# Layer 2 of a hybrid decoder on one core: S5's kernel taps on quarters of the array, and the input projection begun with three tiles over all tokens

## The chip, the cores and the metric

The kernel runs on one core of a Trainium2 chip. The metric is the device time of one execution in microseconds, as the median of several runs.

## What is computed

Two layers of a decoder over 544 tokens (a prompt of 512 and 8 samples of 4), model width 1024, all in float32. Cut to what matters here:

```python
mod = jax.nn.silu(c) @ w['w_mod'] + w['b_mod']
sh1, sc1, g1, sh2, sc2, g2 = jnp.split(mod[:, None, :], 6, axis=-1)
h = _rmsnorm(x, w['norm1_g']) * (1 + sc1) + sh1
z = h @ w['w_in']
zq, zk, zv, zu, za, zg = jnp.split(z, [o1, o2, o3, o4, o5], axis=-1)
...
bu_re = jnp.einsum('gpc,blgc->blgp', bb_re, u)
bu_im = jnp.einsum('gpc,blgc->blgp', bb_im, u)
acc_r, acc_i, sb_r, sb_i = lax.associative_scan(_complex_affine_combine, (a_re, a_im, bu_re, bu_im), axis=1)
...
y = jnp.einsum('gcp,blgp->blgc', c_re, h_re) - jnp.einsum('gcp,blgp->blgc', c_im, h_im)
y = y + d_skip * u
```

Each layer has this mixer (attention with a window of 128, an S5 state-space group of 256 channels, a convolution group of 256 channels, one output projection) and a SwiGLU feed-forward part (FFN) with a width of 2816.

## The kernel before

**Matmuls.** Activations stand with channels on the partitions and tokens on the free axis, in two halves of 272 tokens. Every weight and every activation is split into a high and a low part, and a product is three matmuls of 128x272 (`mm3`, line 603: high by high, high by low, low by high; in the trace their weights are called hi_s and lo_s). A weight chunk of 512 KB arrives as raw_s; `split` (line 584) casts it to hi_s and subtracts for lo_s, on ACT or DVE and on DVE or GpSimd (POOL). Each output tile of 128 columns and one half takes a PSUM bank, and `mtiles` (line 608) goes through the contraction (k) on the outside, over its halves and tiles inside.

**Input projection.** `project(ms)` (line 1090) computes the column tiles in `ms`. With three tiles it runs one stretch over both halves, in six banks; otherwise a stretch over the first half and one over the second. `STEPS` (line 219) sets, for each layer, in which steps the tiles are projected and where the S5, convolution (c0, c1) and attention parts stand among them; `COLS` names the tiles. In layer 2 the tiles 0, 1, 2 are u0 and u1 (S5's input) and q4 (the keys), 3 and 4 belong to the convolution.

**What the projection needs first.** `stat_tile` (line 685) squares a tile of x on ACT (w_s<-x) and adds it to acc_s; `rstd_of` (line 712) sums acc_s over the channels with one-column matmuls, goes through a chain of 12 small operations on DVE (rs_s, three columns wide) and broadcasts the result over the partitions with three matmuls (ps_s<-cst,rs_s), once for each half. `make_h` (line 734) then makes the projection's activations: a product on DVE (w_s<-x,ps_s), scale and shift on ACT, a cast on ACT and a subtraction on DVE, for each k and half. The scale and shift come from w_mod by the adaLN matmuls (mod_s<-wm_s,silu_c), done in steps of four that are spread over the program; their weights (wm_s) are loaded two chunks at a time.

**S5's parameters.** `ssm_params(l)` (line 816) makes the matrices of S5 from the parameters; layer 2's are made during layer 1's FFN. Its last part, `taps` (line 926), computes the kernel taps kk, a table of 128x128 (position and channel, by channel), from mb (two tables of eight 128x128 blocks) and the columns ctr and nct (16 per block): a pair of accumulating matmuls for each block, with the block as weights and 16 columns moving. The result is added to the skip term dm and masked into the weights ssm_tp; then mb is transposed (16 transposes) into ssm_v.

**Order.** All operations are recorded, and a planner (`_schedule`, line 225) puts them in one order by ranks, modelled costs, the tables above and the slots of its buffers. Each engine and DMA queue then runs its own instructions in that order; none overtakes another. Where the planner's model has PE idle for 60 ns or more, it issues a matmul of zeros (a fill, mod_s<-cst,zeros). All operations have line L111 in the trace, so they are told apart by names. PE runs a plain float32 matmul as two records in the trace, a transpose and the split matmuls as one.

## Time and profile before

| | |
|---|---|
| median of 3 runs | 1311.04 us (1310.49 to 1311.4) |
| the profiled execution's own time | 1313.35 us |
| its span in the profile | 1311.5 us (mean granted TensorE clock 0.994) |
| PE busy | 1295.5 us, 99% of the span |
| DVE, ACT, POOL busy | 723.6 us (55%), 431.5 us (33%), 368.6 us (28%) |

The profile is one execution on the chip. A timeline row gives the start and the length of a group of like instructions that follow each other; an x at the row's end counts them, and brackets give the idle time before the group with what ended it. Records of PE overlap, since matmuls are pipelined: what a group costs is read from its start to the next row's start.

### The profile page before, as it was taken

The numbers are of one execution on the slowest core, as the hardware profiler recorded it, in microseconds if no ns is written. First come the engines' busy times: TensorE is split into PE (matmuls) and PEld (weight loads), VectorE is DVE, ScalarE is ACT, GpSimd is POOL, SyncE is SP. The second block draws the span as 40 slices with busy tenths as digits, with TensorE's granted clock in tenths as the row PEclk, the third lists the DMA queues.
The fourth block names the chain that finished last, engine by engine and source line by source line (L and its number), as shares of the span: only waits on it lengthen the run. The fifth ranks groups of instructions, "written<-read, shape, count | busy, mean of one in ns | idle before, by whom it ended". The sixth has DMA issues, their size and how long they took to land.

```text
span 1311.5 us, 25293 instructions
## 1 busy us (share of the span) xinstructions
PE 1295.5 (99%) x10328; PEld 1219.6 (93%) x10328; DVE 723.6 (55%) x1674; ACT 431.5 (33%) x928; POOL 368.6 (28%) x455
## 2 busy tenths in 40 slices
PE   8999999999999999999999999999999999999997
PEld 7888768999999999999988897899999999999997
DVE  6868884676743357433447868657434323344343
ACT  4533471453221122212226346345312112122232
POOL 8653220248432033322012412022223202233101
PEclk9998999999999999999999999999999999999999
DMA  9886785523222223223366672231232222232322
GB/s 333 288 278 210 235 235 197 182 101 97 97 83 96 81 81 97 95 75 105 108 213 233 229 279 69 95 99 49 97 97 96 82 81 83 95 97 81 97 65 69
DMA packets 79654, 176.56 MB, mean 135 GB/s; under 512 B 22769, under 2 KB 40497, under 8 KB 79537
## 3 DMA queue, kind: packets, MB, share of 16 engines
q1 hardware_dynamic: 79536, 174.94, 40.6%
q8 instruction: 81, 1.33, 0.4%
q14 instruction: 37, 0.30, 0.1%
HBM read 164.22 MB, written 10.70 MB: 133 GB/s over the span
## 4 chain that ended last, share of the span: by engine, by line
PE 90%; DVE 3%; DMA 2%; POOL 2%; issue 1%; SPq 1%; ACT 1%; POOLq 0%; ACTq 0%; DVEq 0%
PE ps_s L111 86%; PE mod_s L111 4%; DVE pg_s L111 2%; POOL sp_s L111 1%; SPq L111 1%; POOL pg_s L111 1%; DVE sp_s L111 1%; DMA raw_s<-w_in 1%; DMA wm_s<-w_mod 1%; DMA pg_s<-d_s 0%; DMA conv_out<-pg_s 0%; ACT pg_s L111 0%; DMA pg_s<-ssm 0%; POOL w_s L111 0%; POOLq L1743 0%
## 5 line engine op out<-in xcount | busy, mean ns | idle before, releaser
L111 PE MATMUL ps_s<-pg_s,hi_s 128*128 128x272 f32 x5504 | 1050.8, 290 | 1.4 <-DVE pg_s L111 1.1
L111 PEld LDWEIGHTS ps_s<-pg_s,hi_s 128*128 128x128 f32 x5504 | 865.1, 189 | 18.6 <-issue 13.8
L111 PE MATMUL ps_s<-pg_s,lo_s 128*128 128x272 f32 x2752 | 791.2, 289 | 0.0
L111 PEld LDWEIGHTS ps_s<-pg_s,lo_s 128*128 128x128 f32 x2752 | 518.7, 189 | 7.0 <-issue 6.9
L111 POOL TENSOR_TENSOR lo_s<-raw_s,hi_s 128x1024 fp32r<-128x1024 f32 x77 | 223.3, 2903 | 657.8 <-DVE hi_s L111 372.0
L111 ACT ACTIVATE hi_s<-raw_s 128x1024 fp32r<-128x1024 f32 x128 | 135.0, 1059 | 356.2 <-PE ps_s L111 313.6
L111 DVE TENSOR_TENSOR lo_s<-raw_s,hi_s 128x1024 fp32r<-128x1024 f32 x95 | 119.7, 1261 | 63.9 <-ACT hi_s L111 62.4
L111 DVE TENSOR_TENSOR pg_s<-w_s,pg_s 128x272 fp32r<-128x272 f32 x148 | 113.3, 775 | 37.4 <-ACT pg_s L111 37.0
L111 PE MATMUL ps_s<-pg_s,pg_s 128*128 128x104 f32 (+10 forms) x864 | 123.5, 317 | 2.9 <-DVE nmx_s L111 1.7
L111 ACT ACTIVATE w_s<-ps_s 128x272 f32<-128x272 f32 (+1 forms) x178 | 69.0, 388 | 165.0 <-PE ps_s L111 145.6
L111 PEld LDWEIGHTS ps_s<-pg_s,pg_s 128*128 128x128 f32 (+4 forms) x864 | 97.1, 182 | 27.5 <-issue 12.5
L111 DVE CAST hi_s<-raw_s 128x1024 fp32r<-128x1024 f32 x44 | 30.4, 695 | 157.0 <-PE ps_s L111 157.0
L111 DVE SCALAR_TENSOR_TENSOR x<-ps_s,modT_s,x 128x272 f32<-128x272 f32 (+1 forms) x96 | 45.8, 482 | 105.9 <-PE ps_s L111 105.7
L111 ACT ACTIVATE pg_s<-w_s 128x272 fp32r<-128x272 f32 x149 | 61.7, 426 | 85.0 <-DVE w_s L111 82.6
L111 DVE TENSOR_TENSOR w_s<-w_s,ps_s 128x272 f32<-128x272 f32 x88 | 38.2, 434 | 69.9 <-ACT w_s L111 69.8
L111 ACT ACTIVATE pg_s<-ps_s 128x512 f32<-128x512 f32 (+11 forms) x100 | 35.2, 382 | 65.3 <-PE ps_s L111 63.5
L111 ACT ACTIVATE w_s<-x 128x272 f32<-128x272 f32 x70 | 29.0, 427 | 69.1 <-DVE x L111 61.3
L111 PE MATMUL mod_s<-wm_s,silu_c 128*32 128x512 f32 x320 | 46.9, 616 | 1.4 <-DMA wm_s<-w_mod 1.4
L111 DVE TENSOR_TENSOR acc_s<-acc_s,w_s 128x272 f32<-128x272 f32 x64 | 34.1, 548 | 18.4 <-ACT w_s L111 17.5
L111 POOL TENSOR_TENSOR acc_s<-acc_s,w_s 128x272 f32<-128x272 f32 x5 | 4.6, 912 | 138.8 <-ACT w_s L111 138.7
L111 ACT ACTIVATE w_s<-w_s,modT_s,gain_s 128x272 f32<-128x272 f32 (+1 forms) x64 | 35.9, 591 | 14.3 <-DVE w_s L111 11.3
L111 DVE TENSOR_TENSOR pg_s<-pg_s,pg_s 128x256 f32<-128x256 f32 (+4 forms) x78 | 37.8, 540 | 0.5 <-ACT pg_s L111 0.3
(139 smaller groups left out, 795.3 us busy)
## 6 DMA issues: line engine op xcount, KB each, us to landing
wm_s<-w_mod SPq DMA_DIRECT2D x80, 512.0 KB, 4.6
raw_s<-w_gate SPq DMA_DIRECT2D x44, 512.0 KB, 3.5
raw_s<-w_up SPq DMA_DIRECT2D x44, 512.0 KB, 3.9
raw_s<-w_down SPq DMA_DIRECT2D x44, 512.0 KB, 3.5
raw_s<-w_in SPq DMA_DIRECT2D x24, 512.0 KB, 6.1
pg_s<-cwt SPq DMA_DIRECT2D x20, 512.0 KB, 6.1
pg_s<-w_mod SPq DMA_DIRECT2D x32, 256.0 KB, 6.0
raw_s<-w_out SPq DMA_DIRECT2D x16, 512.0 KB, 4.0
```

Source lines behind the costliest of these rows:

```text
L111: r = real(*a, **k)
```

## The change

Two tables of code change. In layer 2 `taps` exchanges the operands of its matmuls: the 16 columns of ctr or nct, together with the 16 columns of the neighbouring block, are the weights (32 columns, on one quarter of the array, so that the result lands on 32 of 128 PSUM partitions), and the block of mb moves with 128 columns. Four such matmuls on the four quarters are kept together (`order.glue`). The result stands the other way round, so it is copied into a page and transposed back (two transposes of 128x128), and the blocks that count are added to dm in three pieces. The first entry of layer 2's `STEPS` becomes (0, 1, 2), so the projection begins with three tiles over all tokens, where tiles 0 and 1 were projected one by one and half by half, and tile 2 behind the S5 part. The planner's test for free slots is written another way, with the same meaning.

```diff
-         ((0,), (1,), "s5", (2,), (3, 4), "c0", (5,), (6,), (7,), (8,), (9,), "attn", (10, 11), "c1", "norm"))
+         ((0, 1, 2), "s5", (3, 4), "c0", (5,), (6,), (7,), (8,), (9,), "attn", (10, 11), "c1", "norm"))
...
         def taps():
 
-            kp = mbank()
-            for gp in range(8):
-                o = kp[:, gp * 16:(gp + 1) * 16]
-                PE.matmul(out=o, lhsT=mb[0][:, gp].rearrange("p s h c -> p (s h c)"), rhs=ctr[:, gp, :], start=True, stop=False)
-                PE.matmul(out=o, lhsT=mb[1][:, gp].rearrange("p s h c -> p (s h c)"), rhs=nct[:, gp, :], start=False, stop=True)
+            if l == 0:
...
+            else:
+
+                kp = mbank()
+                for b2 in range(2):
+                    for i, c in enumerate((ctr, nct)):
+                        order.glue = ("taps", kp.tensor.name, b2, i)
+                        for q4 in range(4):
+                            gp = 4 * b2 + q4
+                            g0 = min(gp, 6)
+                            PE.matmul(out=kp[32 * q4:32 * q4 + 32, b2 * P:(b2 + 1) * P], lhsT=c[:, g0:g0 + 2, :].rearrange("p g c -> p (g c)"),
+                                      rhs=mb[i][:, gp].rearrange("p s h c -> p (s h c)"), start=i == 0, stop=i == 1, skip_group_check=True)
+                        order.glue = None
+                kt = tmp[0].rearrange("p g s c -> p (g s c)")[:, :2 * P]
+                cp(kt, kp[:, :2 * P])
+                kp = mbank()
+                for b2 in range(2):
+                    PE.transpose(kp[:, b2 * P:(b2 + 1) * P], kt[:, b2 * P:(b2 + 1) * P], ident)
...
-            tt(kk, kp[:, :128], dm, ADD)
+            if l == 0:
+                tt(kk, kp[:, :128], dm, ADD)
+            else:
+                for b2 in range(2):
+                    v = kp[:, b2 * P:(b2 + 1) * P].rearrange("p (g h c) -> p g h c", g=4, h=2)
+                    o = 4 * b2
+                    for g0, m, hh_ in ((0, 4, 0),) if b2 == 0 else ((0, 3, 0), (3, 1, 1)):
+                        d_ = slice((o + g0) * 16, (o + g0 + m) * 16)
+                        tt(kk[:, d_].rearrange("p (g c) -> p g c", c=16), v[:, g0:g0 + m, hh_], dm[:, d_].rearrange("p (g c) -> p g c", c=16), ADD)
```

Since the planner decides, the order moves from the end of layer 1's FFN to the end of layer 2's mixer. PE has 121 fills in place of 104.

PE between the end of layer 1's FFN and the first projection matmuls of layer 2, before: the taps (128x16) with single projection matmuls (128x272) between them, then three fills and the first half's stretch. The broadcast of the second half (rs_s) comes 17 rows behind this piece.

```order
L111 MATMUL ps_s_794_1218<-pg_s_788_646,pg_s_790_633 128x16
L111 MATMUL ps_s_794_1218<-pg_s_752_626,pg_s_789_630 128x16
L111 MATMUL ps_s_1162_1228<-pg_s_1093_1221,hi_s_1079_1175 128x272
L111 MATMUL ps_s_794_1218<-pg_s_788_646,pg_s_790_633 128x16
L111 MATMUL ps_s_794_1218<-pg_s_752_626,pg_s_789_630 128x16
L111 MATMUL ps_s_1200_1230<-pg_s_1093_1221,hi_s_1144_1186 128x272
L111 MATMUL ps_s_794_1218<-pg_s_788_646,pg_s_790_633 128x16
L111 MATMUL ps_s_794_1218<-pg_s_752_626,pg_s_789_630 128x16
L111 MATMUL ps_s_794_1218<-pg_s_788_646,pg_s_790_633 128x16
L111 MATMUL mod_s_0_135<-cst,zeros 128x128 x3
L111 MATMUL ps_s_1157_1223<-pg_s_1093_1221,hi_s_1074_1170 128x272
L111 MATMUL ps_s_1157_1223<-pg_s_1093_1221,lo_s_1075_1173 128x272
```

The same place now, from behind the taps (32x128): fills, the second half's sums (acc_s), the two new transposes, the first half's broadcast, eight fills, an adaLN step, the second half's broadcast, then the projection.

```order
L111 MATMUL ps_s_794_1205<-pg_s_790_633,pg_s_788_646 32x128 x4
L111 MATMUL mod_s_0_135<-cst,zeros 128x128 x2
L111 MATMUL ps_s_1123_1211<-cst,acc_s_561_1118 128x1 x3
L111 MATMUL ps_s_795_1212<-cst,pg_s_787_767 128x128 x2
L111 MATMUL mod_s_0_135<-cst,zeros 128x128 x3
L111 MATMUL ps_s_1102_1188<-cst,rs_s_1104_1203 128x128 x2
L111 MATMUL ps_s_1102_1188<-cst,rs_s_1104_1203 128x16
L111 MATMUL mod_s_0_135<-cst,zeros 128x128 x8
L111 MATMUL mod_s_0_135<-wm_s_1409_1195,silu_c 32x512 x2
L111 MATMUL mod_s_0_135<-wm_s_1410_1196,silu_c 32x512 x2
L111 MATMUL ps_s_1123_1211<-cst,rs_s_1125_1215 128x128 x2
L111 MATMUL ps_s_1123_1211<-cst,rs_s_1125_1215 128x16
```

Both broadcasts now stand ahead of the first projection matmul, and 13 fills stand here.

ACT at the end of layer 1's FFN, before (hi_s_1144 is the cast of the third w_in chunk, hi_s_1160 that of the fourth, w_s_1091<-x_83 the last square of the second half):

```order
L111 ACTIVATE w_s_1088_1184<-x_82 128x272
L111 ACTIVATE hi_s_1144_1186<-raw_s_1143_1176 128x1024
L111 ACTIVATE w_s_1091_1204<-x_83 128x272
L111 ACTIVATE pg_s_748_1197<-ps_s_795_1196 128x512
L111 ACTIVATE hi_s_1160_1210<-raw_s_1159_1181 128x1024
```

and now (1145 and 1159 are these two casts, w_s_1092 the square):

```order
L111 ACTIVATE w_s_1089_1182<-x_82 128x272
L111 ACTIVATE hi_s_1145_1186<-raw_s_1144_1176 128x1024
L111 ACTIVATE hi_s_1159_1197<-raw_s_1158_1179 128x1024
L111 ACTIVATE w_s_1092_1206<-x_83 128x272
L111 ACTIVATE pg_s_748_1192<-ps_s_796_1191 128x512
```

The fourth chunk's cast stands ahead of the square instead of behind it. On DVE that chunk's subtraction (lo_s) now stands ahead of the last add of the second half (acc_s); here is what follows there, the second half's chain (rs_s_1124 to 1126) beside the taps' three adds (pg_s_788) and the first masked copies:

```order
L111 TENSOR_SCALAR rs_s_1124_1213<-ps_s_1123_1211 128x3
L111 SCALAR_TENSOR_TENSOR rs_s_1104_1203<-rs_s_1105_1204,rs_s_1104_1203 128x3
L111 TENSOR_SCALAR rsi_s_1127_1214<-rs_s_1124_1213 128x3
L111 TENSOR_TENSOR pg_s_788_646<-ps_s_795_1212,pg_s_788_646 128x64
L111 TENSOR_SCALAR rs_s_1125_1215<-rsi_s_1127_1214 128x3
L111 TENSOR_TENSOR pg_s_788_646<-ps_s_795_1212,pg_s_788_646 128x48
L111 TENSOR_TENSOR pg_s_788_646<-ps_s_795_1212,pg_s_788_646 128x16
L111 SCALAR_TENSOR_TENSOR rs_s_1126_1216<-rs_s_1124_1213,rs_s_1125_1215 128x3
L111 TENSOR_SCALAR pg_s_745_622<-pg_s_788_646,cst 32x8x16
L111 TENSOR_TENSOR rs_s_1126_1216<-rs_s_1126_1216,rs_s_1125_1215 128x3
L111 TENSOR_SCALAR pg_s_745_622<-pg_s_788_646,cst 32x8x16
L111 SCALAR_TENSOR_TENSOR rs_s_1125_1215<-rs_s_1126_1216,rs_s_1125_1215 128x3
```

Before, the sums and this chain came ahead of the taps' add, and the chain ran beside the first half's products.

## Rows read from the trace of the kernel before

**Rows 1.** The page: the span, and busy time of each engine.

```profile
span 1311.5 us, 25293 instructions
...
PE 1295.5 (99%) x10328; PEld 1219.6 (93%) x10328; DVE 723.6 (55%) x1674; ACT 431.5 (33%) x928; POOL 368.6 (28%) x455
```

**Rows 2.** Windows: us, busy us (instructions) of PE, PEld, DVE, ACT, POOL; PEclk, DMA, GB/s.

```profile
500.00:600.00 100.00, 100.00 (x801) 100.00 (x800) 44.45 (x67) 20.90 (x39) 28.02 (x10) 1.00 0.26 85
...
685.73:689.15 3.42, 3.42 (x34) 3.42 (x33) 2.33 (x7) 3.25 (x6) 1.71 (x1) 1.00 0.95 287
689.15:692.56 3.41, 3.41 (x32) 3.41 (x32) 3.41 (x13) 3.41 (x9) 3.04 (x8) 1.00 0.94 317
692.56:695.97 3.41, 3.41 (x18) 3.41 (x17) 3.21 (x10) 3.15 (x8) 1.13 (x2) 0.50 0.70 284
```

**Rows 3.** Timeline of PE: start us, us, line, operation, out<-in, xcount.

```profile
676.25 1.07 PE L111 MATMUL mod_s<-wm_s,silu_c 128*32 128x512 f32 x8
677.25 0.52 PE L111 MATMUL ps_s<-pg_s,hi_s 128*128 128x272 f32 x2
...
683.65 1.88 PE L111 MATMUL mod_s<-wm_s,silu_c 128*32 128x512 f32 x8
685.46 0.66 PE L111 MATMUL ps_s<-cst,pg_s 128*128 128x128 f32 x4
...
686.54 0.82 PE L111 MATMUL ps_s<-cst,rs_s 128*128 128x128 f32 x6
687.21 0.85 PE L111 MATMUL ps_s<-cst,pg_s 128*128 128x128 f32 x6
687.90 1.86 PE L111 MATMUL ps_s<-pg_s,pg_s 128*128 128x16 f32 x16
...
691.77 0.91 PE L111 MATMUL mod_s<-cst,zeros 128*128 128x128 f32 x6
692.44 0.47 PE L111 MATMUL ps_s<-pg_s,hi_s 128*128 128x272 f32 x1
...
696.05 0.29 PE L111 MATMUL ps_s<-pg_s,lo_s 128*128 128x272 f32 x1
```

**Rows 4.** Timeline of PE at the kernel's start: a modulation group on quarters.

```profile
13.67 0.64 PE L111 MATMUL mod_s<-pg_s,silu_c 128*32 128x128 f32 x16
14.24 0.83 PE L111 MATMUL ps_s<-cst,acc_s 128*128 128x1 f32 x6
```

**Rows 5.** Timelines of SyncE and ACT, and the landing times of raw_s in 660 to 700 us.

```profile
678.25 0.38 SPq L111 DMA_DIRECT2D raw_s<-w_in  x1
...
684.06 0.43 ACT L111 ACTIVATE w_s<-x 128x272 f32<-128x272 f32 x1 [3.49 <-DVE rs_s L111]
...
686.32 1.05 ACT L111 ACTIVATE hi_s<-raw_s 128x1024 fp32r<-128x1024 f32 x1
...
DMA to landing us min/median/max: 3.4/5.5/7.5
```

**Rows 6.** Timeline of DVE at the same place.

```profile
680.60 1.23 DVE L111 TENSOR_TENSOR lo_s<-raw_s,hi_s 128x1024 fp32r<-128x1024 f32 x1 [0.51 <-ACT hi_s L111]
682.24 0.16 DVE L111 TENSOR_SCALAR rs_s<-ps_s 128x3 f32<-128x3 f32 x1 [0.41 <-PE ps_s L111]
...
684.52 0.44 DVE L111 TENSOR_TENSOR acc_s<-acc_s,w_s 128x272 f32<-128x272 f32 x1
```

**Rows 7.** Timelines of PE and DVE: S5, and the attention's wait.

```profile
726.11 0.29 PE L111 MATMUL ps_s<-pg_s,lo_s 128*128 128x272 f32 x1
726.51 3.94 PE L111 MATMUL ps_s<-pg_s,pg_s 128*128 128x136 f32 x32
...
754.64 3.94 DVE L111 TENSOR_TENSOR pg_s<-pg_s,pg_s 128x256 f32<-128x256 f32 x10
...
794.48 0.70 PE L111 MATMUL ps_s<-pg_s,pg_s 64*128 64x256 f32 x2 [0.82 <-DVE nmx_s L111]
```

**Rows 8.** The page's groups: PE's small matmuls; busy, mean, idle before and its releaser.

```profile
L111 PE MATMUL ps_s<-pg_s,pg_s 128*128 128x104 f32 (+10 forms) x864 | 123.5, 317 | 2.9 <-DVE nmx_s L111 1.7
```

More of the change, by code (lines that the diff above doesn't have):

```diff
@@ L338, in _schedule, with placeable @@
     lock = {}
+    needs = [[(n, tags[n][0], nth[n]) for n in t] for t in touch]
+    def placeable(i):
+        for n, t, m in needs[i]:
+            if n not in held:
+                f = len(free[t])
+                if not f or f <= RESERVE.get(t, 99) and f <= bisect.bisect_left(todo[t], m):
+                    return False
+        return True
     pick, why, last_dep, slot_by, freed_by, prev_end, prev_op = [0] * N, {}, {}, {}, {}, {}, {}
@@ L365, in _schedule @@
                 for r, i in pool[e]:
-                    if not all(len(free[tags[n][0]]) > min(bisect.bisect_left(todo[tags[n][0]], nth[n]), RESERVE.get(tags[n][0], 99))
-                               for n in touch[i] if n not in held):
+                    if not placeable(i):
                         continue
@@ L387, in _schedule @@
                         best = (key, r, i, p)
+                    if e != "ACT":
+                        break
                 if best is None and e == "PE" and FILL and spare and NWU <= issued < reals and now >= at[e] + (0.0 if filled else FILL):
@@ L926, in taps @@
         def taps():
-            kp = mbank()
-            for gp in range(8):
-                o = kp[:, gp * 16:(gp + 1) * 16]
-                PE.matmul(out=o, lhsT=mb[0][:, gp].rearrange("p s h c -> p (s h c)"), rhs=ctr[:, gp, :], start=True, stop=False)
-                PE.matmul(out=o, lhsT=mb[1][:, gp].rearrange("p s h c -> p (s h c)"), rhs=nct[:, gp, :], start=False, stop=True)
+            if l == 0:
+                kp = mbank()
+                for gp in range(8):
+                    o = kp[:, gp * 16:(gp + 1) * 16]
+                    PE.matmul(out=o, lhsT=mb[0][:, gp].rearrange("p s h c -> p (s h c)"), rhs=ctr[:, gp, :], start=True, stop=False)
+                    PE.matmul(out=o, lhsT=mb[1][:, gp].rearrange("p s h c -> p (s h c)"), rhs=nct[:, gp, :], start=False, stop=True)
+            else:
[11 more added lines that the diff above has]
+                cp(kt, kp[:, :2 * P])
+                kp = mbank()
+                for b2 in range(2):
+                    PE.transpose(kp[:, b2 * P:(b2 + 1) * P], kt[:, b2 * P:(b2 + 1) * P], ident)
             kk = bb[:, 512:640]
```

## The prediction

> **What bounds the kernel now.** I read the page's summary first: TensorE (PE) is busy 99% of the span [rows 1]. So time is saved only by giving PE less to do, by letting it run at its higher clock, or by removing one of its few waits; VectorE (DVE) and ScalarE (ACT) matter only where PE comes to wait for them. Next the table by windows [rows 2]: in 500 to 600 us PE issues 801 matmuls in 100 us, 0.125 us each, with no gap. The three windows behind it show the place of this change: the granted clock is 1.00 until 692.56 and 0.50, the lower of the two levels, from there to 695.97 where layer 2's input projection begins. What PE did before the clock fell stands in its timeline [rows 3]: transposes, one-column sums, and the 16-column tap matmuls. Three sizes are read there, each as the distance from a start to the next row's start:
>
> - The taps. From 687.90 to 691.77, less three stray projection matmuls of 0.125: 3.5 us for 32 records, 0.11 each.
> - The half clock. From 692.44 to 696.05, 16 projection matmuls in 3.61 us; at 0.125 they take 2.0. Lost: 1.6 us.
> - A late load of w_mod. The eight records at 683.65 last 1.81 us; the same eight at 676.25 last 1.00. Lost: 0.8 us.
>
> The profiled execution took 1313.35 us with a span of 1311.5, and lies 2.3 above the median of 1311.04. I sum the change against it and take the difference over to the median. About 0.2%, 2.6 us, is what a measurement can tell from no change.
>
> **The change part by part.**
>
> *Taps.* The 16 instructions (32 records) with 16 moving columns go: -3.5. In their place come 16 with 32 columns of weights, 128 moving columns, on quarters of the array. No row of before has them with these operands; the nearest is the modulation at the kernel's start, also 32 columns of weights and 128 moving, where a group of 16 records lasts 0.64 us [rows 4], so 32 take 1.3. The bounds are 1.1 (the next row starts 0.57 after that group's start) and 3.5 (quarters do not overlap, 0.11 each as in the old taps). I take 1.3, since shape and tiling are the same. The sum for this part: -2.2. The Trainium skill, "TensorEngine Tiling (Array Packing)", Performance Considerations, gives up to 4 times for a swap of the two operands with at most 32 columns; by it the taps would take an estimated 0.9 and the total would come out 0.4 lower. No run has shown that yet.
>
> *Copy, transposes and adds.* Two more transposes on PE at 0.115 (from 687.21 to 687.90, six records) [rows 3]: +0.2. The copy out of PSUM is one more ACT operation. It lies beside PE's fills and the second half's sums, so I cost it at nothing; without that cover it would be about 0.4, as ACT's square of nearly the same size [rows 5]. The three adds in place of one are two more operations on DVE; where they stand is counted with DVE below.
>
> *Fills.* The order has 17 more zero matmuls (121 for 104): 13 before the first projection matmul, where 4 stood around there, 9 at the end of S5, where 2 stood, and one later. One takes 0.22 (three from 691.77 to 692.44 [rows 3]): +3.8. They are issued whether or not there is anything to wait for, so I count all of them as work and below only what a wait lasts beyond them.
>
> Work: -2.2 + 0.2 + 3.8 = **+1.8**.
>
> *What goes of the old losses.* The half clock came right after the 16-column taps, and these are gone: -1.6. The bounds are 0 and -1.6; I take the whole, since the granted clock was still 1.00 behind the transposes at 685.46 and 687.21 and the broadcast between them [rows 2, 3]. The late w_mod: in the new order the step at this place uses a pair of chunks whose loads stand one earlier in the queue: -0.8 (0 if the next w_mod pair, now behind the hist and rope transfers, is late instead). Together **-2.4**.
>
> *What is late next: the start of the projection.* Before, PE could begin with the first half's tokens while the second half's statistics were still being made. Now three tiles run over all tokens, and the order puts the broadcast of the second half's rstd ahead of the first projection matmul. That needs the last square (ACT), the last add into acc (DVE), three one-column sums (PE) and the chain of 12 small operations (DVE). On ACT the cast of the fourth w_in chunk now stands ahead of that square, and on DVE its subtraction ahead of the add. The step by step: this chunk was issued at 678.25 and its cast began at 686.32 [rows 5]; the queue landed such chunks in 3.4 to 7.5 us, so it lands between 681.7 and 685.8, and I take 684, near the median of 5.5. Cast 1.05 to 685.05, subtraction 1.23 to 686.3, add 0.44 to 686.7 [rows 5, 6]; the rest of the first half's chain, six operations at 0.2 that wait on each other (682.24 is such a one), to 687.9. Then 24 DVE operations from the second chain's start to its end, with the taps' three adds and five normalisations between. They last from 0.16 (as 682.24) to 0.44 (as 684.52) and overlap in pairs; I estimate 0.19 each, 4.6 us, to 692.5. Broadcast 0.67 (686.54 to 687.21), so the projection starts at 693.2.
>
> By PE's own work it would start as follows. The FFN ended at 682.9 (683.65 less six transposes). Less 1.0 for the adaLN step that leaves the FFN's last tiles (as at 676.25), and 0.4 for the first sums, counted next: 681.5. Then two sets of sums at 0.6 (685.46 to 686.54, less four transposes), 18 transposes 2.1, taps 1.3, 13 fills 2.9, two adaLN steps 2.0, two broadcasts 1.3: 10.8, to 692.3. The wait is the difference: **+0.9**, with the bounds 0 (the chunk lands at 681.7, and PE's own work sets the time) and +2.7 (685.8).
>
> *DVE and ACT inside the stretch.* With six banks a k step lasts 18 matmuls, 2.3 us, and each needs both halves' activations: four DVE operations of 0.4 [rows 6], four on ACT of the same order, with the weights' casts between. That is nearly as long. I take **+0.5** (0 to 1).
>
> *S5's end.* The DVE chain from the first copy to its last row (754.64 + 3.94) ends 32 us after the first input matmul of S5 at 726.51 [rows 7]. In the new order PE has about 5 us less work between that matmul and the first outputs; the first outputs need only groups that DVE finishes before its last scans, the last set needs the end. With the nine fills counted, PE gets there about when DVE ends: **+0.3** (0 to 1).
>
> Total: 1.8 - 2.4 + 0.9 + 0.5 + 0.3 = +1.1: 1314.4 for an execution like the profiled one, **1312.1** on the median.
>
> **The rivals.**
>
> *Faster: no new wait.* The chunk lands near 681.7, DVE keeps ahead in the stretch, S5 ends in time, and the wait of 0.82 that PE has for the softmax maximum [rows 7] goes with its smaller companions (1.7 in all in the page's group [rows 8]), as the query tiles shift; so does the 0.3 by which 726.51 comes later than 0.125 after 726.11 [rows 7]. Then -0.6 - 1.7 - 0.3 = -2.6: 1308.4. For it: PE hardly waited anywhere before. Against it: the order shows a longer chain ahead of the first matmul, and fills mark where gaps are expected. Chance 0.20, of which some 0.12 goes beyond the bound.
>
> *Slower: head of the line.* The fourth chunk lands as late as before or later. ACT and DVE run in order, so the square and the add behind the cast and the subtraction wait with them, though the three tiles don't need that chunk at all. At 685.8 the start moves by 1.8 more: 1313.9; at 687, 1315.1. It decides from a landing later than about 685.5. For it: DMA was moving 317 GB/s there, 0.94 busy [rows 2]. Against it: 7.5 is the longest of its stretch. Chance 0.18, at 1314.3.
>
> *The clock falls all the same.* The gap of the new order still has 18 transposes, one-column sums, and waits. If the first 16 projection matmuls again run at 0.226, the 1.6 is not gained: 1313.7. Rows speak against it (clock 1.00 through the old transposes). The Trainium skill, "TensorE: Matmul & The Clock Gate", Part 4 (PE-mode transpose), says that a transpose does not count as PE being busy in the same way; by it the gap would be thinner than it looks and the low level would return. The trace agrees in so far only as the clock did fall after this stretch, though not right behind the transposes. Chance 0.08.
>
> *The change doesn't do what it says.* The quarters run one after another and the new taps cost the old 3.5: 2.2 more, 1314.3. Against it: the row for the same shape. Chance 0.06.
>
> **How the numbers follow.** Forecast 0.48, rivals 0.20, 0.18, 0.08 and 0.06. The range runs from 1308.4, the faster rival's time, to 1315.6, past the late chunk's. Faster than 1308.4: 0.13, nearly all the first rival. Slower than 1313.7: 0.13 from the late chunk, 0.04 from the clock, 0.05 from the quarters and 0.03 from the forecast's own upper end: 0.25. Same: 0.62.
>
> **What would show it.** In the profile of the changed kernel: taps as 32 records within 1.3 us; 242 records of fills; a granted clock of 1.00 through the first projection matmuls; PE idle before the second half's broadcast or the first projection matmul, released by DVE's rs_s or pg_s; the cast of the fourth chunk ahead of the last square on ACT; short waits of the S5 outputs for DVE. The forecast is wrong if PE has no gap there (faster), if the cast starts after 685.5 (slower), or if the clock shows 0.50 again.

## The result and the profile after

| | before | after |
|---|---|---|
| median of runs taken side by side | 1311.22 us (4 runs, 1310.49 to 1312.08) | 1321.55 us (4 runs, 1320.07 to 1322.87) |
| the profiled execution's own time | 1313.35 us | 1320.07 us |
| its span (mean granted TensorE clock) | 1311.5 us (0.994) | 1318.3 us (0.998) |

The ratio is 1.0068, with an interval of 1.0051 to 1.0085. The change makes the kernel 10.3 us slower by the medians and 8.9 by the ratio (6.7 to 11.1). That lies within 2%, but far outside the 0.2% that the prediction called no change, and above its range.

The page of the changed kernel, its span and the busy time of each engine:

```profile
span 1318.3 us, 25379 instructions
...
PE 1298.1 (98%) x10364; PEld 1220.7 (93%) x10364; DVE 728.3 (55%) x1678; ACT 431.2 (33%) x927; POOL 369.3 (28%) x455
```

Against [rows 1], PE has 36 more records: 17 fills (two records each) and two transposes. It is busy for 2.6 us more, in a span that is 6.8 us longer. So most of the loss is PE waiting.

The two profiled executions differ before the changed place too. At 98 to 106 us the granted clock was 0.57 in the one of before and 1.00 in the one of after. The order there is the same in both, so this isn't the change. After reaches the end of layer 1's FFN (its first one-column sums) at 679.83, before at 681.10. From there to the span's end after takes 638.5 us and before 630.4: the change costs 8.1 us in these two executions.

To see where, I cut this part at the starts of rows that both traces have: the first sums at the FFN's end, the first S5 input matmul (128x136), the first S5 output, the first convolution matmul (128x104), layer 2's first FFN sums, and PE's last record. In each stage I summed what PE issues at the durations that undisturbed rows show (0.125 a matmul with 272 columns, 0.22 a fill, 1.0 an adaLN step). The stage's time less that sum is what PE lost, to waits and to the clock:

| lost, us | start and first stretch | S5's input to its first output | to the convolution | to layer 2's FFN | the FFN | sum | PE's work |
|---|---|---|---|---|---|---|---|
| before | 3.2 | 0.6 | 1.9 | 3.2 | 2.0 | 11.0 | 612.1 |
| after | 5.1 | 2.3 | 5.1 | 3.1 | 1.7 | 17.3 | 613.9 |
| after, profiled again | 5.2 | 2.9 | 3.8 | 3.5 | 1.7 | 17.2 | 613.9 |

The work grows by 1.8, as in the prediction's sum. The rest, 6.3, is lost time, in the first three stages. The traces show it as follows.

**The start.** The timeline of PE in the changed kernel, from the FFN's end to the first projection matmuls and two places behind them, where [rows 3] stood (start us, us, line, operation, out<-in, xcount, idle before and what ended it):

```profile
680.98 1.06 PE L111 MATMUL mod_s<-wm_s,silu_c 128*32 128x512 f32 x8
681.98 1.53 PE L111 MATMUL ps_s<-cst,pg_s 128*128 128x128 f32 x12
683.43 1.08 PE L111 MATMUL ps_s<-pg_s,pg_s 128*32 128x128 f32 x32
684.45 0.71 PE L111 MATMUL mod_s<-cst,zeros 128*128 128x128 f32 x4
...
687.31 0.84 PE L111 MATMUL ps_s<-cst,rs_s 128*128 128x128 f32 x6 [0.53 <-DVE rs_s L111]
688.00 2.03 PE L111 MATMUL mod_s<-cst,zeros 128*128 128x128 f32 x16
689.96 1.06 PE L111 MATMUL mod_s<-wm_s,silu_c 128*32 128x512 f32 x8
691.47 0.84 PE L111 MATMUL ps_s<-cst,rs_s 128*128 128x128 f32 x6 [0.44 <-DVE rs_s L111]
692.16 0.50 PE L111 MATMUL ps_s<-pg_s,hi_s 128*128 128x272 f32 x2
...
696.84 0.40 PE L111 MATMUL ps_s<-pg_s,hi_s 128*128 128x272 f32 x1 [0.18 <-DVE pg_s L111]
...
698.67 0.36 PE L111 MATMUL ps_s<-pg_s,hi_s 128*128 128x272 f32 x1 [0.56 <-DVE w_s L111]
```

The taps take 1.02 us (683.43 to 684.45), where they took 3.5. The two broadcasts wait 0.53 and 0.44 for DVE in spite of the 13 fills, and the first stretch waits 0.18 and 0.56 for its activations. The half clock of [rows 2] is gone, as the table by windows of the changed kernel shows (us; busy us and records of PE; PEclk; DMA share; GB/s):

```profile
676.00:692.00 16.00, 15.03 (x146) 1.00 0.95 319
692.00:798.00 106.00, 103.43 (x772) 1.00 0.67 218
```

DVE's timeline in the changed kernel shows what held the first broadcast:

```profile
683.31 1.22 DVE L111 TENSOR_TENSOR lo_s<-raw_s,hi_s 128x1024 fp32r<-128x1024 f32 x1
684.45 0.43 DVE L111 TENSOR_TENSOR acc_s<-acc_s,w_s 128x272 f32<-128x272 f32 x1
684.80 0.35 DVE L111 SCALAR_TENSOR_TENSOR rs_s<-rs_s,rs_s 128x3 f32<-128x3 f32 x2
685.98 0.23 DVE L111 TENSOR_TENSOR pg_s<-pwe_s,pg_s 128x64 f32<-128x64 f32 x1 [0.82 <-DMA pg_s<-st]
```

DVE stands 0.82 us in front of an S5 operation whose input, the layer's state, is still in transfer (st). The rest of the first half's chain (rs_s) is queued behind it. The fourth chunk, from which the prediction expected the delay, was in time, as ACT's timeline of the changed kernel shows, in its cast, the square behind it, and ACT's next cast of a chunk:

```profile
681.73 1.06 ACT L111 ACTIVATE hi_s<-raw_s 128x1024 fp32r<-128x1024 f32 x1 [1.71 <-DMA raw_s<-w_in]
682.70 0.41 ACT L111 ACTIVATE w_s<-x 128x272 f32<-128x272 f32 x1
...
715.52 1.06 ACT L111 ACTIVATE hi_s<-raw_s 128x1024 fp32r<-128x1024 f32 x1 [0.67 <-PE ps_s L111]
```

**The loads.** The same rows show the second thing: from the fourth chunk's cast to the next one pass 33.8 us, where before it was 21.5 (686.32 to 707.81). The stretch over all tokens uses three chunks until its end, and the fourth is the next step's, so none comes free. The loads follow: SyncE's timeline of the kernel before, then of the changed one, the last issue of a w_in chunk ahead of this pause and the first behind it:

```profile
689.84 0.33 SPq L111 DMA_DIRECT2D raw_s<-w_in  x1
...
712.34 0.38 SPq L111 DMA_DIRECT2D raw_s<-w_in  x1
```

```profile
684.34 0.92 SPq L111 DMA_DIRECT2D raw_s<-w_in  x2
...
719.08 0.34 SPq L111 DMA_DIRECT2D raw_s<-w_in  x1
```

The last row ahead of the pause in the changed kernel holds two issues, the second at 684.82. So the pause lasts 34.3 us instead of 22.5. Behind it six chunks follow within 28 us (719.08 to 746.68), before six in 39 (712.34 to 751.12). The table by windows of the kernel before, then of the changed one (us; busy us and instructions of PE, PEld, DVE, ACT, POOL; PEclk; DMA share; GB/s):

```profile
692.00:716.00 24.00, 24.00 (x178) 21.05 (x178) 19.12 (x65) 16.23 (x38) 3.79 (x4) 0.93 0.57 191
732.00:748.00 16.00, 16.00 (x127) 13.39 (x120) 16.00 (x35) 4.57 (x9) 6.62 (x5) 1.00 0.63 214
```

```profile
692.00:716.00 24.00, 23.15 (x175) 19.43 (x174) 15.18 (x51) 13.41 (x32) 3.11 (x4) 1.00 0.45 143
732.00:748.00 16.00, 15.18 (x120) 13.09 (x119) 13.54 (x30) 5.77 (x15) 6.70 (x7) 1.00 1.01 273
```

DMA moves less in the first window (143 GB/s for 191), and in the second it is busy throughout (share 1.01, was 0.63). The adaLN weights land there too. The landing times of wm_s in 690 to 765 us, of before and then of the changed kernel:

```profile
DMA to landing us min/median/max: 3.6/4.4/5.8
```

```profile
DMA to landing us min/median/max: 3.5/5.2/8.8
```

They were not issued later: the pair for the step at 746.70 left at 739.12, 7.6 us ahead of it, and before the pair for the step at 745.30 left at 739.70, 5.6 us ahead. PE waits for them, in its timeline of the changed kernel:

```profile
729.36 1.05 PE L111 MATMUL mod_s<-wm_s,silu_c 128*32 128x512 f32 x4
730.70 1.05 PE L111 MATMUL mod_s<-wm_s,silu_c 128*32 128x512 f32 x4 [0.28 <-DMA wm_s<-w_mod]
731.68 0.39 PE L111 MATMUL ps_s<-pg_s,lo_s 128*128 128x272 f32 x1
...
746.70 1.05 PE L111 MATMUL mod_s<-wm_s,silu_c 128*32 128x512 f32 x4 [0.60 <-DMA wm_s<-w_mod]
747.97 1.05 PE L111 MATMUL mod_s<-wm_s,silu_c 128*32 128x512 f32 x4 [0.22 <-DMA wm_s<-w_mod]
748.95 0.40 PE L111 MATMUL ps_s<-pg_s,hi_s 128*128 128x272 f32 x1
```

The idle times in brackets are only a part of it: a step of eight records, 1.00 us where nothing disturbs it, lasts 2.32 at 729.36 and 2.25 at 746.70. The first of these two stands ahead of S5's input, so it is in the first column of the table and not in the second. Summed over all adaLN steps between 678 and 766 us, what goes beyond 1.00 each, with the idle time ahead of the step, is 0.8 us before (the step at 683.65), 3.2 in the changed kernel and 4.5 in its second profile; the wait for rs_s behind one of these steps is not counted.

**Attention.** PE's timeline of the kernel before, ahead of [rows 7]'s last row. The 32 records are 16 of scores (64 rows) and 16 of another product with 272 columns that stands among them:

```profile
785.68 5.97 PE L111 MATMUL ps_s<-pg_s,pg_s 64*128 64x128 f32 x32
```

The same place in the changed kernel, where the scores come in pieces between projection matmuls, and the table by windows around its longest wait (PE alone):

```profile
783.83 0.71 PE L111 MATMUL ps_s<-pg_s,pg_s 64*128 64x128 f32 x6
...
785.27 0.49 PE L111 MATMUL ps_s<-pg_s,pg_s 64*128 64x128 f32 x2 [0.41 <-DVE nmx_s L111]
...
793.44 1.46 PE L111 MATMUL ps_s<-pg_s,pg_s 64*128 64x128 f32 x10
795.10 0.48 PE L111 MATMUL ps_s<-pg_s,pg_s 64*128 64x128 f32 x2 [0.20 <-DVE nmx_s L111]
...
799.50 0.81 PE L111 MATMUL ps_s<-pg_s,pg_s 64*128 64x256 f32 x2 [1.18 <-DVE nmx_s L111]
```

```profile
798.00:802.00 4.00, 2.82 (x12) 0.74 0.01 4
802.00:806.00 4.00, 4.00 (x28) 0.83 0.01 2
```

The wait for the softmax maximum is 1.18 instead of 0.82, and two pieces of the scores wait 0.41 and 0.20 for it, which before did not wait. All of PE's waits for nmx_s last 2.7 us in the list of waits, where they lasted 1.7 [rows 8]. In both, 0.87 of this stands in layer 1 (between 159 and 179 us), so in layer 2 the waits grow from 0.82 to 1.80. In this execution the clock fell behind the wait: the 13 projection records from 800.24 to 803.35 take 3.11 us, 1.5 more than at 0.125 each.

### The profile page after: what moved, and what is told of

It is laid out like the page before. It is cut to its first block, busy times and chain, and to the rows that moved or that the text cites. A ratio compares the mean times of both kernels' runs of the same rounds, so it can differ in the third digit from the quotient of the medians.

```text
span 1318.3 us, 25379 instructions
## 1 busy us (share of the span) xinstructions
PE 1298.1 (98%) x10364; PEld 1220.7 (93%) x10364; DVE 728.3 (55%) x1678; ACT 431.2 (33%) x927; POOL 369.3 (28%) x455
## 4 chain that ended last, share of the span: by engine, by line
PE 86%; DVE 4%; DMA 4%; POOL 2%; issue 1%; SPq 1%; ACT 1%; POOLq 0%; ACTq 0%; DVEq 0%
PE ps_s L111 82%; PE mod_s L111 4%; DVE pg_s L111 2%; DMA wm_s<-w_mod 2%; POOL sp_s L111 1%; SPq L111 1%; DMA raw_s<-w_in 1%; DVE sp_s L111 1%; DVE w_s L111 1%; POOL pg_s L111 1%; DMA conv_out<-pg_s 0%; ACT pg_s L111 0%; DMA pg_s<-d_s 0%; DVE lo_s L111 0%; DMA pg_s<-st 0%
## 5 line engine op out<-in xcount | busy, mean ns | idle before, releaser
L111 PE MATMUL ps_s<-pg_s,pg_s 128*128 128x104 f32 (+10 forms) x864 | 120.1, 316 | 5.0 <-DVE nmx_s L111 2.7
L111 PEld LDWEIGHTS ps_s<-pg_s,pg_s 128*128 128x128 f32 (+4 forms) x864 | 93.7, 178 | 27.8 <-issue 11.8
L111 DVE TENSOR_TENSOR pg_s<-pg_s,pg_s 128x256 f32<-128x256 f32 (+4 forms) x78 | 42.8, 604 | 0.7 <-ACT pg_s L111 0.4
```

Source lines behind the costliest of these rows:

```text
L111: r = real(*a, **k)
```

## The experiments

A ratio is to runs of the kernel before on the same chip; 0.1% is 1.3 us. Beside experiments 1 to 4 the kernel before had a median of 1313.46, beside 5 to 7 of 1312.58, beside 8 to 11 of 1313.95.

**1. The taps alone.** The changed kernel with the old steps.

```diff
-         ((0, 1, 2), "s5", (3, 4), "c0", (5,), (6,), (7,), (8,), (9,), "attn", (10, 11), "c1", "norm"))
+         ((0,), (1,), "s5", (2,), (3, 4), "c0", (5,), (6,), (7,), (8,), (9,), "attn", (10, 11), "c1", "norm"))
```

> The changed kernel with the old first steps of layer 2 (tiles 0 and 1 one by one, half by half); only the taps' exchange of operands is left. Its order has 152 fills, before 104, the changed kernel 121. Theory 1 (the loss belongs to the three tiles over all tokens: a start that waits for both halves' statistics, DVE just in time, loads that come late): no such waits here, 1309 to 1313, if the 48 further fills stand where PE would wait anyhow. Theory 2 (fills are work that is paid in full): 48 x 0.22 = 10.6, less 2.4 for the taps, about 1319.

Measured: 1327.2 us, ratio 1.0100 (1.0068 to 1.0132). Slower than the whole change, and than either theory said. The planner put 152 fills into this order, 48 more than before: PE's work is 8.6 us more, and 15.4 are lost, where before loses 11.0. The taps by themselves are still short here, so a shorter piece of work has led to a longer order. The edit of the operands can't be priced from this run, since the order changed with it. Late w_mod loads are in it too, without a stretch over three tiles: its adaLN steps between 678 and 766 us last some 3 us in all beyond 1.00 each.

**2. The steps alone.** The kernel before with the new steps and its old taps.

```diff
-         ((0,), (1,), "s5", (2,), (3, 4), "c0", (5,), (6,), (7,), (8,), (9,), "attn", (10, 11), "c1", "norm"))
+         ((0, 1, 2), "s5", (3, 4), "c0", (5,), (6,), (7,), (8,), (9,), "attn", (10, 11), "c1", "norm"))
```

> The kernel before with the new steps of layer 2 alone, the taps as they were. 114 fills. Theory 1 (the three tiles over all tokens cost the time): 1319 to 1323, as the changed kernel. Rival (the exchange of the taps' operands and what it moves costs it): 1311 to 1314.

Measured: 1322.62 us, ratio 1.0062 (1.0042 to 1.0082), as slow as the whole change. The lost time is 14.9, by stage 2.8, 2.9, 3.6, 3.3 and 2.3: S5 and attention lose what they lose in the changed kernel. So the step with three tiles, in the order that the planner makes with it, costs the 10 us, and in the timed runs the new taps give back nothing that can be measured beside it.

**3. Short loads of w_mod.** The changed kernel's own order; its last 20 loads of w_mod take 64 of 1024 columns.

```diff
+                if "in_" in k and "w_mod" in str(getattr(k["in_"].tensor, "name", "")) and k["out"].tensor.name.startswith("wm_s"):
+                    self.nwm = getattr(self, "nwm", 0) + 1
+                    if self.nwm >= 61:
...
+                        k = dict(k, out=k["out"][:, :, :64], in_=k["in_"][:, :, :64])
```

> The changed kernel in its own order, but each of the last 20 loads of w_mod (from the adaLN step ahead of the projection on) brings 64 of 1024 columns, and the adaLN matmuls read these again and again, so layer 2's modulation for the FFN is not that of the reference. Theory (late loads in 700 to 750 us are part of the loss): the adaLN steps' waits, about 1.8 us by the intervals of the trace, go, and the w_in chunks land earlier: 1318 to 1320. Rival (the late loads only take the place of waits that come anyhow): 1321 to 1322.

Measured: 1318.68 us, ratio 1.0030 (1.0015 to 1.0046). The landing times of wm_s in 690 to 765 us in this run:

```profile
DMA to landing us min/median/max: 1.6/2.2/5.8
```

PE no longer waits for wm_s in that stretch, and the S5 stage loses 0.4 where the changed kernel loses 2.3 and 2.9. From the FFN's first sums to PE's last record this execution takes 628.0 us, the changed kernel's 631.1. By the medians the late loads cost some 5 us of the 10, by these two profiles 3.1, if taking them away is free in the kernel before. Experiment 6 tests that.

**4. Without the 13 fills.** The changed kernel's order; the fills 64 to 76, ahead of the first projection matmul, aren't issued.

```diff
+                if isinstance(k.get("lhsT"), bass.AP) and k["lhsT"].tensor.name.startswith("zeros"):
+                    self.nz = getattr(self, "nz", 0) + 1
+                    if 64 <= self.nz < 77:
+                        continue
```

> The changed kernel in its own order without the 13 fills ahead of the first projection matmul. The fills are 2.9 us of PE. Theory (PE waits there for DVE's chain in any case): the time stays within 0.6 of the changed kernel's 1321.5, and the waits for rs_s grow to some 3.5 us in all. Rival (fills are paid work): 1318.6. If the granted clock falls for want of them, up to 2 us more than the theory says.

Measured: 1323.14 us, ratio 1.0068 (1.0051 to 1.0085), the same as with them. PE's timeline at the start of the projection in this run (the line of all operations is L115 here, since the edit moves it; in the kernels below it is another one again):

```profile
688.19 0.80 PE L115 MATMUL ps_s<-cst,acc_s 128*128 128x1 f32 x6 [0.30 <-DVE rs_s L115]
...
690.35 0.84 PE L115 MATMUL ps_s<-cst,rs_s 128*128 128x128 f32 x6 [1.09 <-DVE rs_s L115]
...
693.52 1.05 PE L115 MATMUL mod_s<-wm_s,silu_c 128*32 128x512 f32 x4 [1.34 <-DMA wm_s<-w_mod]
```

2.9 us of work are gone, and 3.5 more are lost. Not all of it is lost here: from the first sums to S5's input this execution takes 53.2 us, where the changed kernel takes 54.3 and 54.5, so 1.1 to 1.3 us of the fills came back at this place and were lost again behind it. The waits for rs_s come to 1.4 and not to the 3.5 expected; with them PE waits 1.34 for w_mod. So the greater part of these fills covered waits, for DVE's chain and for a load, and the time shows no gain from leaving them out.

**5. The attention's wait filled.** The changed kernel with six more fills ahead of the matmul that waits 1.18, in layer 2's attention (hence 1.3 us more work). It ran beside the unaltered changed kernel.

```diff
+                lt = k.get("lhsT")
+                if isinstance(lt, bass.AP) and lt.shape[0] == 64 and k["out"].shape[-1] == 256:
+                    self.n256 = getattr(self, "n256", 0) + 1
+                    if self.n256 == 28:
...
+                        for j in spare[:6]:
+                            f_, fa, fk = self.calls[j][0]
+                            f_(*fa, **fk)
```

> The changed kernel once more, unaltered, so that the next ones are compared with it on the same chip: 1.005 to 1.0085 of the kernel before. In its profile the four stages behind layer 1's FFN should lose as before: late w_mod steps between S5's input and its outputs, and some 5 us between those and the attention's end.

> The changed kernel in its own order with six more fills ahead of the score matmul at which PE waited 1.18 us for the softmax maximum and behind which the granted clock was 0.50 for some 4 us. Theory (the idle gap let the clock fall): the fills lie in the gap, the clock stays at 1.00, and 1.3 to 1.5 us are saved. Rival (the clock falls for what PE did before the gap, or would have fallen anyhow): no gain, up to 0.3 slower.

Measured: the changed kernel again 1322.84 us, ratio 1.0079 (1.0065 to 1.0093); with the fills 1320.84, ratio 1.0065 (1.0050 to 1.0081). The intervals overlap. The windows around the wait, of the changed kernel profiled again, in which the place lies some 4.6 us later:

```profile
798.00:802.00 4.00, 3.80 (x25) 1.00 0.00 0
802.00:806.00 4.00, 2.83 (x18) 1.00 0.02 4
806.00:810.00 4.00, 4.00 (x34) 1.00 0.00 2
```

Here the same wait (1.17 at 804.13) is followed by a clock of 1.00, without any fill. So the fall in the first profile is not in every execution; it explains the 5.1 against 3.8 lost in this stage. With the fills it stayed at 1.00 too. The other profiles say more. The same matmul waits 1.17 to 1.19 in experiments 3, 4, 7 and 8, which have no fills there, and in all four the clock is 0.57 to 0.66 in the 4 us behind it. So it fell in five of six executions without the fills, at a cost of 1.2 to 1.5 us, and in none of the three with them (5, 9 and 10). That speaks for the theory, but nine executions are few, and in experiment 2, with another order, the same wait of 1.18 was followed by 1.00.

**6. The control for 3.** The kernel before, with the same 20 loads cut by the same lines.

> The kernel before with the same 20 loads of w_mod cut to 64 of 1024 columns as in the run that cut them in the changed kernel; so layer 2's modulation for the FFN is not that of the reference. Theory (late loads are a part of the loss that the new order made): the kernel before gains at most 1 us, its one late step of 0.8, while the changed kernel gained some 4 to 5. Rival (either kernel is held up by these loads alike): it gains 4 or more too, 1306 to 1308.

Measured: 1312.22 us, ratio 0.9993 (0.9979 to 1.0007). Its losses sum to 10.1, before's to 11.0. In the old order these loads cost at most 1 us, so the rest of what experiment 3 won is a cost that the new order makes: some 4 us by the medians, whose intervals are about 2 us to either side, and 2.2 by the profiles, in which this kernel gains 0.9 of 623.1 from the first sums on.

**7. DVE's head of the line.** The changed kernel, with the two DVE products that read S5's state moved behind the second half's chain.

```diff
+            at = max(n for n, i in enumerate(seq) if "_1125_" in name(i, "out")) + 1
+            late = [i for i in seq[:at] if name(i, "in0").startswith(("pwe", "pg_s6_1174_")) and name(i, "out").startswith("pg_s6_1174_")]
+            seq = [i for i in seq[:at] if i not in late] + late + seq[at:]
```

> The changed kernel in its own order, but the two DVE products that read the S5 state (pg_s<-pwe_s,pg_s) stand behind the second half's chain. In the trace DVE waited 0.82 us for the state's transfer there, in the middle of the first half's chain, with the second half's chain behind it. Theory (that transfer, and not the fourth chunk's cast, is the head of the line at the projection's start): both broadcasts come 0.8 to 1.2 us earlier, and the time falls by as much. Rival (the cast and subtraction set it, or DVE in the stretch takes it back): under 0.4.

Measured: 1320.57 us, ratio 1.0066 (1.0051 to 1.0081), against 1.0079 for the unaltered kernel beside it; the intervals overlap. PE's timeline in this run:

```profile
691.08 0.74 PE L119 MATMUL ps_s<-cst,rs_s 128*128 128x128 f32 x6
691.67 2.03 PE L119 MATMUL mod_s<-cst,zeros 128*128 128x128 f32 x16
693.63 2.09 PE L119 MATMUL mod_s<-wm_s,silu_c 128*32 128x512 f32 x8
695.65 0.84 PE L119 MATMUL ps_s<-cst,rs_s 128*128 128x128 f32 x6
```

The broadcasts no longer wait for rs_s. Counted from the first sums they come 0.6 and 0.2 us earlier than in the changed kernel's first profile and 1.1 and 1.8 earlier than in its second; the theory said 0.8 to 1.2. But the adaLN step between them, 1.06 in the changed kernel, lasts 2.09: PE got there earlier and its weights had not landed. The wait has moved from DVE to a load. The profiled execution, the slowest of its six, gains nothing from the first sums on (631.4 us for 631.1).

**8. Short loads of w_in.** The changed kernel's order; from the 17th on, its chunks of w_in take 64 columns (the last 8), and the casts and subtractions read these 64 repeated. w_mod is loaded whole.

```diff
+                if "in_" in k and "out" in k and "w_in" in str(getattr(k["in_"].tensor, "name", "")) and k["out"].tensor.name.startswith("raw_s"):
+                    self.nraw = getattr(self, "nraw", 0) + 1
+                    if self.nraw >= 17:
...
+                        k = dict(k, out=k["out"][:, :64], in_=k["in_"][:, :64])
```

> The changed kernel in its own order, all of w_mod loaded, but the last 8 w_in chunks of layer 2 bring 64 of 1024 columns, and the casts and subtractions read these again and again, so layer 2's projections from the fifth tile on are not those of the reference. Theory (the w_mod loads are issued in time and land late because w_in chunks that the three-tile stretch held back arrive at the same time): w_mod lands in 4 to 5 us, and most of what cutting w_mod gained is gained here too: 3 to 5 us, 1.003 to 1.005 of before. Rival (w_mod is issued late, or is slow by itself): under 1 us.

Measured: 1319.87 us, ratio 1.0048 (1.0030 to 1.0065). The second window, and the landing times of wm_s, in this run:

```profile
732.00:748.00 16.00, 16.00 (x130) 14.04 (x129) 11.32 (x27) 5.27 (x12) 4.40 (x6) 1.00 0.73 189
```

```profile
DMA to landing us min/median/max: 3.6/4.7/6.3
```

Nothing about w_mod was altered, yet its longest landing falls from 8.8 to 6.3 us, and the S5 stage loses 0.4, as in experiment 3. The adaLN steps between 678 and 766 us last in all only 0.2 us beyond 1.00 each, where it is 3.2 and 4.5 in the changed kernel. What makes w_mod late there is the w_in traffic in the same stretch. The kernel before was not run with the same loads cut, so the gain in time, 4 us by the medians, has no control.

**9. Two mendings together.** The edits of 5 and 7.

> The changed kernel with both small mendings: six fills at the softmax wait, and the S5 state's products behind the chain. Nothing left out. If the two are separate parts of the loss, 1.0075 less 0.0014 and 0.0013: 1.0045 to 1.0055 of before. If they gain by the same thing, 1.0065.

Measured: 1321.59 us, ratio 1.0062 (1.0046 to 1.0078). No better than each alone, so the sum that was expected did not come. The stages show why only in part: from S5 to the convolution it loses 2.5 (3.8 and 5.1 in the changed kernel), but S5 still loses 3.0, from the loads, and PE has the 1.3 us of the six fills.

**10. All three.** The edits of 5, 7 and 3.

> Both small mendings, and the last 20 w_mod loads cut to 64 of 1024 columns (layer 2's modulation for the FFN is not that of the reference). If the three parts make up the loss: 0.9995 to 1.0015 of before. If a part of the loss lies elsewhere (in the fills and the moved work themselves), 1.002 to 1.004.

Measured: 1316.89 us, ratio 1.0032 (1.0017 to 1.0047); the profiled span is 1314.0. By stage it loses 3.3, 0.4, 2.6, 3.1 and 1.7, together 11.1, which is what before loses (11.0). So the three parts make up the lost time in this execution, the fastest of its nine. What remains against before is PE's work, 3.0 us: 23 more fills (5.1) less what the taps save. The ratio lies where the second expectation put it. The timed runs show no gain over experiment 3 alone, though.

**11. Another order of the old steps.** The kernel before with other weights for the planner, which give another order with 98 fills.

```diff
-dict(s5=116e3, attn=64e3, norm=93e3, c1=170e3)
+dict(s5=124e3, attn=34e3, norm=93e3, c1=230e3)
...
-LOCK, RESERVE = 140.0
+LOCK, RESERVE = 200.0
```

> The kernel before with its code and steps, only three of the planner's numbers altered (lifts of s5, attention and c1, the bank lock), which gives another order with 98 fills. Theory (what counts is where the waits fall, and an order with no three-tile stretch has no reason to lose): 0.997 to 1.003. Rival (the numbers of before suit its order alone, so any other order loses): 1.004 or more.

Measured: 1313.42 us, ratio 0.9998 (0.9984 to 1.0012). This other order costs nothing by itself, so the 10 us are not the price of every new order. It is one order, though: that of experiment 1, with the old steps too, has a ratio of 1.0100. No version that ran is faster than the kernel before beyond its interval.

## Why the prediction was wrong

The forecast was 1312.1 and the result 1321.55. Two steps of its sum failed. The late w_mod was taken as a gain of 0.8, and the loads became later: the adaLN steps lose 2.4 to 3.7 us more than before. The attention was put at nothing, and its stage loses 1.9 to 3.2 us more. Point by point, by the prediction's own steps:

- **Taps: right.** 1.02 us was measured, where 1.3 was taken from [rows 4]; that is a little below the lower bound of 1.1. The Trainium skill, "TensorEngine Tiling (Array Packing)", Performance Considerations, led to an estimate of 0.9; the trace lies between the two, nearer to the page.
- **The half clock: right.** The first projection matmuls run at 0.125 with a clock of 1.00. All profiles bear it out. The four with the 16-column taps (before and experiments 2, 6 and 11) have a clock of 0.53 to 0.69 in 692 to 696 us; the ten with the new taps have 1.00 from 684 to 704 us, also experiment 1, which has the old steps. So in these orders the fall goes with the taps and not with the steps. The rival by which transposes would bring the low level back did not come. The Trainium skill, "TensorE: Matmul & The Clock Gate", Part 4 (PE-mode transpose), was cited for it; in this trace the clock is 1.00 from 676 to 798 us, with 18 transposes close together, so the fall that the rival drew from the page did not come. How transposes by themselves count, no run shows.
- **Fills: the sum was right.** The count was right, 242 records, and so was the sum of the work, +1.8, to which only the waits beyond the fills were added. But experiment 4 shows that a kernel without the 13 at the start isn't faster: the greater part of them marks time in which PE would wait. So the +3.8 is no price of the fills themselves; the place to look for a cost was what they wait for.
- **The start: right in time, wrong in the cause.** 693.2 was forecast for the first projection matmul; it came at 692.16. The FFN of this execution ended 1.3 us earlier; counted from its first sums, 12.1 was forecast and 12.3 measured (13.9 in the second profile, where the adaLN step between the broadcasts lasts 2.23). The two waits for rs_s make up 0.97, near the +0.9. The fourth chunk's cast stood ahead of the square, as the order said, and did no harm, since it began at 681.73, at the early bound. That was luck: the load took 6.3 us, more than the 5.75 of the forecast, but it was issued at 675.33, where the forecast used the old kernel's 678.25. What held DVE was the transfer of S5's state. The rival "head of the line" named the right mechanism at the wrong instruction.
- **DVE in the stretch: somewhat too low.** +0.5 was taken (0 to 1); the two waits of 0.18 and 0.56 are 0.74.
- **The late w_mod: the step failed, and it is the largest.** The sum took -0.8 for a load that would be earlier, and only a bracket, 0 if the next w_mod pair were late instead. The step at the start was in time in the first profile (1.06 at 689.96), though not in the second. The next ones were late in both: the adaLN steps lose 3.2 and 4.5 us where before they lost 0.8, and experiments 3 and 6 put the cost that the new order adds by late loads at about 4 us by the medians. I looked at one load at the change's place and never asked when buffers come free for the chunks that follow. The order suggests it: three chunks are in use until a stretch of 30 us ends. Then the held chunks and w_mod share the DMA (share 1.01), which experiment 8 shows.
- **S5's end: +0.3 was taken for a wait on DVE; what PE waited for there were the loads,** which were not in that step.
- **Attention: costed at nothing, and by the faster rival as a gain of 1.7.** The wait grew from 0.82 to 1.18, all of nmx_s from 1.7 to 2.7, and this stage loses 1.9 to 3.2 us more than before. The query tiles did shift, and the scores with them, into pieces that wait for the maximum; which of the shifts lengthened the wait was not tried. The larger of the two numbers has the fall of the clock in it, which five of six executions show (experiment 5). The faster rival's -1.7 was misread besides: 0.87 of it are waits of layer 1, which the change doesn't touch.

What stays open. Late w_mod loads are in experiment 1 as well, so the stretch over three tiles is not the only order that makes them. The lost time of the first stage is 5.1 and 5.2 in the two profiles of the changed kernel and 3.5 in experiment 5, which has the same order there. So its share of the 10 us is not better known than 0.3 to 2. Why the mendings of experiment 9 don't add is not settled. And that the held weight buffers are what pushes w_in together with w_mod is read from the casts, the issues and the windows; a kernel with one more weight buffer was not run, so that link is argued, while the collision itself is shown. The two profiles also differ by less (8.1 from 680 us on) than the medians (10.3), though within the interval of the ratio.

## What to carry to other kernels

When a step takes more tiles at once, follow its buffers to the end of the stretch: the loads that can't start meanwhile come later, together with others, and a load that nobody touched becomes the late one. Fills in a planned order are also a map of expected waits: leaving out 13 of them gained nothing here, so price what stands behind them. And where one step of a planned order moves, look at every wait that the new order shows, as far as a hundred microseconds on.

## What the hardware showed beyond that

- The same place of the same order had a different clock in different executions: at 98 to 106 us 0.57 in the profile of before, 0.64 in the second of the changed kernel, 1.00 in its first; behind the softmax wait 0.74 and 0.83 in one and 1.00 in the other. A fall that one profile shows is worth further profiles before it is explained: behind this wait it was in five of six.
- Behind the taps with 16 moving columns the granted clock fell in four of four profiles, and behind the new taps in none of ten.
- Exchanging the operands, with quarters of the array, took the taps from 3.5 to 1.02 us for the same 32 records, a factor of 3.4.
- Loads of 512 KB (wm_s, 690 to 765 us) landed after 4.4 us in the median, at most 5.8, before, and after 5.2, at most 8.8, in the changed kernel. The DMA share in 732 to 748 us was 0.63 and 1.01.
